# A hybrid decoder block on one core: halves of h stored side by side, and the first depth half of MLP units two to four in 512-column matmuls

## The chip, the core and the metric

The kernel runs on one core of a Trainium2 chip. The metric is the device time of one launch in microseconds; where a kernel was run several times, the median. A core has five engines that run side by side and meet through semaphores: TensorE (PE in the profile, with its weight loads shown apart as PEld), VectorE (DVE), ScalarE (ACT), GpSimd (POOL) and SyncE (SP, which here issues nearly all the loads). Each engine takes its instructions in the order in which they were written into its own list.

## The reference, cut to what matters

One decoder block in float32 on 256 positions and a width of 2048: an adaLN modulation computed from c, an S5 state-space branch beside block attention, a gated merge, and a squared-ReLU MLP of width 8192. The change lies in the MLP's first product; the layout of the first normed h changes too.

```python
mod = c_act @ w_ada[l] + b_ada[l]
sh1, sc1, g1, sh2, sc2, g2 = [m[:, None, :] for m in jnp.split(mod, N_MOD, axis=-1)]
...
h2 = rms_norm(x, norm_mlp_g[l]) * (1.0 + sc2) + sh2
x = x + g2 * (jnp.square(jax.nn.relu(h2 @ w_ff1[l])) @ w_ff2[l])
```

## The kernel before

Every float32 product is made from two rounded parts: a = a_hi + a_lo, and the product is taken as hi*hi + hi*lo + lo*hi. A weight tile of 128 x 1024 numbers (512 KB) is loaded by SP into one of seven buffers `wraw`. ACT casts it to `whi` (line 161) and DVE subtracts to get `wlo` (line 163); of each of these there are four buffers. `stream` does this ahead of the matmuls, under a raised priority. The activations h are held the same way, as a high half `ah` and a low half `al` of one buffer `a2` (tag A2), written by `make_h1` for the first sub-layer and by `make_h` for the MLP (in the trace: `ah` and `h2h`).

Two helpers multiply with a weight tile as the stationary operand, so that the result comes out transposed (hidden units on the partitions, 256 positions along the columns):

- `gemm_t` (lines 190 to 207) takes one depth tile of 128 rows and 1024 hidden units. Each block of 128 units gets three matmuls of 256 columns: whi with the high half of h, whi with the low half, wlo with the high half (lines 201, 202, 203). Two blocks share a bank of PSUM, four banks hold the result. One weight tile costs 24 matmuls.
- `gemm_d` (lines 209 to 231) takes two depth tiles and 512 hidden units. Each block gets one matmul of 512 columns, whi with both halves of h (line 219), and one of 256, wlo with the high half (line 223). A block has a bank to itself, with the products of the high half and of the low half in its two halves; they are added when the bank is emptied. One weight tile costs 8 + 8 matmuls. In a group's last weight tile the blocks are finished one after the other.

PSUM has eight banks: five (tag mm) for these results, three (tag ax) for small things. While the first depth half runs, a group of four takes four of the five; from the second depth half on, groups take turns between the two kinds.

The MLP has eight units of 1024 hidden units. For the first four (NP), the first part of the depth (kt 0 to 7; for the first unit kt 0 to 3) is computed early, in the loop `for g in range(NP)`, and its result is kept in SBUF in a tile `part`, because the rest of h is not yet there. The first unit runs on h before its scaling by 1/rms and is scaled by DVE afterwards (line 1470). In this loop the lane "ada" gives, per weight tile, RM = 0.85 further tiles of the modulation weights (`in_wat_dram`): SP loads them into the same seven buffers and DVE multiplies and sums each (line 314, called an adaLN sum here). They yield the scale and shift without which the second part of h cannot be made. Also in this loop lie four broadcasts (`ada_bcast`, line 400) and 16 transposes for that second part (`make_h`, line 759). Then `ff1` computes the rest of the depth with `gemm_d`, adds `part` (lines 1360 and 1361), applies the squared ReLU, and `ff2` multiplies with the second weight.

The order of the instructions on each engine is fixed when the program is built: a scheduler picks, by priorities and by its own estimate of when things are ready, so the lists differ from the order of the code. In particular it may let PE do several weight tiles on one bank before it goes on to the next bank, when it believes the next bank is still being emptied.

Of the kernel before, what the change touches and what calls it, by code (L numbers as in the profile page):

```python
# [13 lines left out]
F32R = mybir.dt.float32r  # L14
# [5 lines left out]
P = 128  # L20
S = 256
D = 2048
KT = D // P
# [54 lines left out]
class Kern:  # L78
# [130 lines left out]
    def gemm_d(self, src, kts, c0, x2):  # L209
        nc = self.nc  # L210
        banks = self.four("pd")
        pairs = self.pairs(list(kts))
        n = len(pairs)
        for i, (ks, hi, lo) in enumerate(self.stream(src, pairs, c0)):
            last = i == n - 1
            cut = lambda blk, k: slice(512 * k + blk * P, 512 * k + (blk + 1) * P)

            def high(blk, k):
                nc.tensor.matmul(banks[blk], hi[:, cut(blk, k)], x2[:, :, ks[k], :], start=i + k == 0, stop=False,  # L219
                                 skip_group_check=True)  # L220

            def low(blk, k):
                self.mm = nc.tensor.matmul(banks[blk][:, S:2 * S], lo[:, cut(blk, k)], x2[:, 0, ks[k], :], start=False,  # L223
                                           stop=last and k == 1, skip_group_check=True)

            for blks in [(b,) for b in range(4)] if last else [range(4)]:
                for f in (high, low):
                    for blk in blks:
                        for k in range(2):
                            f(blk, k)  # L230
        return banks
# [694 lines left out]
    def body(self):  # L926
        nc, a, v = self.nc, self.a, self.nc.vector
# [25 lines left out]
        A2, B2 = self.col("A2", KT), self.col("B2", KT)  # L953
# [36 lines left out]
        win = a["w_in"][0]  # L990
        with self.tc.high_priority(offset=OF1):
            self.norm1()
            a2 = self.slot("A2", [P, 2, KT, S], F32R, name="ah")
            self.ah, self.al = a2[:, 0], a2[:, 1]
            parts0 = modn(0)
            for units, fold, last in parts0:
                for ld, tot in units:
                    ld()
            totals(parts0)
            self.scale1(0, n=1)  # L1000
            self.make_h1(0, A1, B1, 1)
            self.gates = [(None, self.acopy)]
            for i in range(4):
                self.ada_bcast(rc[:, 4 * i:4 * i + 4], self.cb[:, i * 512:(i + 1) * 512], turn=False)
            self.ssm_params()
# [176 lines left out]
        for i in range(1, 4):  # L1182
# [3 lines left out]
            banks = self.gemm_n(win, range(KT), c0, self.ah, self.al, mid={8: to_ssm} if i == 1 else {})  # L1186
# [32 lines left out]
        banks = self.gemm_t(a["w_glu"][0], range(8), 0, yy[:, 0], yy[:, 1])  # L1219
# [24 lines left out]
        for cg in range(2):  # L1244
            banks = self.gemm_n(a["w_proj_ssm"][0], range(8), cg * 1024, gg[:, 0], gg[:, 1])
# [14 lines left out]
        for cg in range(2):  # L1260
# [6 lines left out]
            banks = self.gemm_n(a["w_out"][0], range(KT), cg * 1024, mh, ml, tail=TW if cg else 1)  # L1267
# [22 lines left out]
        with self.hot():  # L1290
            ss2 = self.col("ss2", 2)
            self.pin(v.reduce_sum(ss2, sq.rearrange("p (t c) -> p t c", t=2), axis=AX.X))
            rs2 = self.rstd(ss2, 2, "r2")
            a2 = self.slot("A2", [P, 2, KT, S], F32R, name="h2h")
            self.ah, self.al = a2[:, 0], a2[:, 1]
            s0 = scale2(0, 0, None)
            s1 = scale2(1, 0, s0)
        self.gates = [(None, None)] * 4 + [(s1, self.sq_last)] * 2
# [34 lines left out]
        w1, w2 = a["w_ff1"][0], a["w_ff2"][0]  # L1333
# [122 lines left out]
        self.lanes["ada"][1] = 0.0  # L1456
        for g in range(NP):
            part = self.slot(("S4", "T", "SV", "S5")[g], [P, 4, 512], name="part")
            if g:
                banks = self.gemm_t(w1, range(0, 8), g * 1024, self.ah, self.al)  # L1460
            else:
                wh, wl = [self.slot(n, [P, 4, 1024], F32R, name="wf") for n in ("VT", "QT")]
                banks = self.gemm_t(w1, range(0, 4), 0, hp[:, 0], hp[:, 1], mid={2: h_first, 3: h_second},
                                    homes=[(wh[:, k, :], wl[:, k, :]) for k in range(4)])
            for b in range(4):
                if g:
                    nc.scalar.copy(part[:, b, :], banks[b])
                else:
                    with self.after(hs["h0"]):
                        v.tensor_mul(part[:, b, :].rearrange("p (k s) -> p k s", s=S),  # L1470
                                     banks[b].rearrange("p (k s) -> p k s", s=S),
                                     self.R[:, None, :].to_broadcast([P, 2, S]))
            parts.append(part)
            if g == 0:
                self.lanes["ada"][1] = RM
                self.agate = None
            if g == 1:
                scale2(2, 0, self.done[-1][0])
                scale2(3, 0, self.done[-1][0])
                self.ada_bcast(B2[:, 0:4], b2r, self.mm)  # L1480
# [63 lines left out]
```

## Time and profile before

| what | value |
|---|---|
| time, median of 3 runs | 1387.89 us (1386.99 to 1388.09) |
| the profiled execution's own time | 1388.54 us |
| its span, first to last instruction | 1386.8 us |
| mean granted TensorE clock | 0.995 |
| matmuls in the trace | 8338 |
| the loop over the first depth half, units two to four | 676.3 to 748.8 us |

The profile's first part gives each engine's busy time, its share of the span and its instructions. A row of a timeline reads: start in us, duration in us, engine, line, operation, what is written and from what, shape, count, and in brackets how long the engine was idle before it and what ended that. Ends of matmuls are modelled, so that successive rows of PE overlap; the distance between starts is the pace. A row of a table by lines gives total busy time, mean ns of one, idle time before and what ended it. SPq is SP's queue, where the loads are issued.

### The profile page before, as it was taken

The page shows a single profiled execution, that of the slowest core. Times are in us where ns is not written, and L with a number is a line of the kernel's source. Part 1 is how long each engine was busy: PE and PEld are TensorE (multiplying, and loading weights), DVE is VectorE, ACT ScalarE, POOL GpSimd, SP SyncE. Part 2 cuts the span into 40 slices and gives each one's busy share as a digit, 9 for nine tenths or more (in the row PEclk, how much of TensorE's full clock was granted, in tenths as well). Part 3 has the DMA queues.
Part 4 walks back from the last instruction along what each step waited for, and adds up shares of the span by engine and source line. Part 5 has one row for each costly group of instructions (what it writes and reads, how often), then busy time and mean ns, then how long its engine had stood idle before and what let it go on. Part 6 is the DMA issues. An engine that isn't in the chain of part 4 may idle for free.

```text
span 1386.8 us, 21589 instructions
## 1 busy us (share of the span) xinstructions
PE 1354.2 (98%) x8338; PEld 1173.9 (85%) x8338; DVE 1061.6 (77%) x1481; ACT 709.7 (51%) x956; POOL 42.6 (3%) x96
## 2 busy tenths in 40 slices
PE   6999999999999999999999999999999999999997
PEld 5888898988788898788999888888888888888885
DVE  6699998788798898987886976777666555555677
ACT  4464356346646743446455655444453453634543
POOL 1000000400002100000000000000000000000000
PEclk9999999999999999999999999999999999999999
DMA  9999965888457889898597878797878656566561
GB/s 372 380 403 370 338 218 169 267 297 316 138 177 218 303 289 338 286 398 289 195 378 236 292 243 253 246 256 279 254 233 241 206 187 197 183 195 195 176 202 66
DMA packets 112422, 356.43 MB, mean 257 GB/s; under 512 B 12240, under 2 KB 12272, under 8 KB 111904
## 3 DMA queue, kind: packets, MB, share of 16 engines
q1 hardware_dynamic: 109280, 348.96, 74.5%
q0 software_dynamic: 2896, 5.83, 1.4%
q8 instruction: 65, 1.06, 0.3%
q10 hardware_dynamic: 144, 0.26, 0.1%
q14 instruction: 37, 0.30, 0.1%
HBM read 350.79 MB, written 2.51 MB: 255 GB/s over the span
## 4 chain that ended last, share of the span: by engine, by line
PE 84%; DVE 7%; DMA 4%; ACT 3%; issue 1%; SPq 0%; DVEq 0%; ACTq 0%
PE pn L253 15%; PE pn L254 14%; PE pn L255 14%; PE pd L219 13%; PE pd L223 7%; PE pt L202 5%; PE pt L201 5%; PE pt L203 5%; DVE wlo L163 2%; DVE wraw L314 1%; DMA wraw<-in_w_out_dram 1%; DMA wraw<-in_w_proj_ssm_dram 1%; ACT whi L161 1%; PE ys L908 1%; PE rk L723 1%
## 5 line engine op out<-in xcount | busy, mean ns | idle before, releaser
L161 ACT CAST whi<-wraw 128x1024 fp32r<-128x1024 f32 x448 | 468.1, 1051 | 547.2 <-PE pn L254 222.2
L163 DVE TENSOR_TENSOR wlo<-wraw,whi 128x1024 fp32r<-128x1024 f32 x448 | 545.7, 1224 | 238.4 <-ACT whi L161 231.5
L219 PE MATMUL pd<-h2h,whi 128*128 128x512 f32 x800 | 208.9, 393 | 0.0
L253 PE MATMUL pn<-whi,ff 128*128 128x512 f32 x496 | 193.0, 389 | 0.0
L254 PE MATMUL pn<-whi,ff 128*128 128x512 f32 x496 | 193.0, 389 | 0.0
L255 PE MATMUL pn<-wlo,ff 128*128 128x512 f32 x496 | 191.6, 389 | 0.0
L219 PEld LDWEIGHTS pd<-h2h,whi 128*128 128x128 f32 x800 | 140.5, 189 | 21.7
L314 DVE SCALAR_TENSOR_TENSOR wraw<-wraw,cb 128x1024 f32<-128x1024 f32 x128 | 156.2, 1221 | 0.0
L253 PE MATMUL pn<-whi,ah 128*128 128x512 f32 x320 | 126.4, 398 | 3.3 <-ACT ah L161 1.6
L223 PEld LDWEIGHTS pd<-h2h,wlo 128*128 128x128 f32 x800 | 116.1, 190 | 12.5
L254 PE MATMUL pn<-whi,ah 128*128 128x512 f32 x320 | 125.1, 391 | 0.0
L223 PE MATMUL pd<-h2h,wlo 128*128 128x256 f32 x800 | 119.3, 281 | 0.0
L255 PE MATMUL pn<-wlo,ah 128*128 128x512 f32 x320 | 114.6, 393 | 0.0
L201 PE MATMUL pt<-ah,whi 128*128 128x256 f32 x384 | 106.8, 287 | 6.3 <-ACT ah L161 4.5
L255 PEld LDWEIGHTS pn<-wlo,ff 128*128 128x128 f32 x496 | 93.1, 188 | 19.3
L253 PEld LDWEIGHTS pn<-whi,ff 128*128 128x128 f32 x496 | 93.1, 188 | 19.2
L254 PEld LDWEIGHTS pn<-whi,ff 128*128 128x128 f32 x496 | 93.1, 188 | 19.1
L202 PE MATMUL pt<-ah,whi 128*128 128x256 f32 x384 | 108.3, 287 | 0.0
L203 PE MATMUL pt<-ah,wlo 128*128 128x256 f32 x384 | 104.0, 286 | 1.5 <-DVE wlo L163 1.5
L201 PEld LDWEIGHTS pt<-ah,whi 128*128 128x128 f32 x384 | 73.5, 194 | 7.5 <-ACT ah L161 5.2
L202 PEld LDWEIGHTS pt<-ah,whi 128*128 128x128 f32 x384 | 74.3, 193 | 1.3 <-issue 0.8
L203 PEld LDWEIGHTS pt<-ah,wlo 128*128 128x128 f32 x384 | 71.9, 193 | 2.6 <-DVE wlo L163 2.3
(377 smaller groups left out, 1992.2 us busy)
## 6 DMA issues: line engine op xcount, KB each, us to landing
wraw<-in_w_ff_dram SPq DMA_DIRECT2D x256, 512.0 KB, 4.9
wraw<-in_w_in_dram SPq DMA_DIRECT2D x128, 512.0 KB, 6.2
wraw<-in_wat_dram SPq DMA_DIRECT2D x128, 512.0 KB, 5.5
ahm<-in_wat_dram SPq DMA_DIRECT2D x48, 512.0 KB, 7.3
wraw<-in_w_out_dram SPq DMA_DIRECT2D x32, 512.0 KB, 6.6
wraw<-in_w_proj_attn_dram SPq DMA_DIRECT2D x16, 512.0 KB, 5.9
wraw<-in_w_proj_ssm_dram SPq DMA_DIRECT2D x16, 512.0 KB, 6.5
ahm<-in_wan_dram SPq DMA_DIRECT2D x8, 512.0 KB, 11.0
```

The lines of the kernel that those rows point to most:

```text
L161: h = self.nc.scalar.copy(hi, src)
L163: s = self.nc.vector.tensor_sub(lo, src, hi.bitcast(F32))
L201: nc.tensor.matmul(o, hi[:, c], xh[:, kx, :], start=st, stop=False, skip_group_check=True)
L202: nc.tensor.matmul(o, hi[:, c], xl[:, kx, :], start=False, stop=False, skip_group_check=True)
L203: self.mm = nc.tensor.matmul(o, lo[:, c], xh[:, kx, :], start=False, stop=sp, skip_group_check=True)
L219: nc.tensor.matmul(banks[blk], hi[:, cut(blk, k)], x2[:, :, ks[k], :], start=i + k == 0, stop=False, skip_group_check=True)
L223: self.mm = nc.tensor.matmul(banks[blk][:, S:2 * S], lo[:, cut(blk, k)], x2[:, 0, ks[k], :], start=False, stop=last and k == 1, skip_group ...
L253: nc.tensor.matmul(o, xh[:, kx, tk], hi[:, c], start=q == 0, stop=False)
L254: nc.tensor.matmul(o, xl[:, kx, tk], hi[:, c], start=False, stop=False)
L255: self.mm = last = nc.tensor.matmul(o, xh[:, kx, tk], lo[:, c], start=False, stop=q == n - 1)
L314: v.scalar_tensor_tensor(w, w, 1.0, self.cb[:, (i % 2) * 1024:(i % 2 + 1) * 1024], op0=OP.mult, op1=OP.mult, accum_out=pc[:, i:i + 1])
L723: nc.tensor.matmul(p[q, k * 64:(k + 1) * 64], nr[q, i, k].rearrange("p s c -> p (s c)"), self.cc[q, i, 8 * b + k].rearrange("p s c -> p (s ...
```

## The change

`a2` is laid out as [partition, depth tile, half, position] instead of [partition, half, depth tile, position], in both places where it is made, so that the two halves of a depth tile lie side by side and the operand of line 219 is one run of 512 columns. The first depth half of MLP units two to four is computed by `gemm_d` in two groups of 512 hidden units each, instead of by one `gemm_t` of 1024. A group's four banks are emptied by an ACT copy of 256 columns and a DVE add of 256 columns each, where before ACT copied each bank whole. The first unit stays as it was.

```diff
--- before.py
+++ after.py
@@ -216,11 +216,11 @@
             cut = lambda blk, k: slice(512 * k + blk * P, 512 * k + (blk + 1) * P)
 
             def high(blk, k):
-                nc.tensor.matmul(banks[blk], hi[:, cut(blk, k)], x2[:, :, ks[k], :], start=i + k == 0, stop=False,
+                nc.tensor.matmul(banks[blk], hi[:, cut(blk, k)], x2[:, ks[k], :, :], start=i + k == 0, stop=False,
                                  skip_group_check=True)
 
             def low(blk, k):
-                self.mm = nc.tensor.matmul(banks[blk][:, S:2 * S], lo[:, cut(blk, k)], x2[:, 0, ks[k], :], start=False,
+                self.mm = nc.tensor.matmul(banks[blk][:, S:2 * S], lo[:, cut(blk, k)], x2[:, ks[k], 0, :], start=False,
                                            stop=last and k == 1, skip_group_check=True)
 
             for blks in [(b,) for b in range(4)] if last else [range(4)]:
@@ -990,8 +990,8 @@
         win = a["w_in"][0]
         with self.tc.high_priority(offset=OF1):
             self.norm1()
-            a2 = self.slot("A2", [P, 2, KT, S], F32R, name="ah")
-            self.ah, self.al = a2[:, 0], a2[:, 1]
+            a2 = self.slot("A2", [P, KT, 2, S], F32R, name="ah")
+            self.ah, self.al = a2[:, :, 0], a2[:, :, 1]
             parts0 = modn(0)
             for units, fold, last in parts0:
                 for ld, tot in units:
@@ -1291,8 +1291,8 @@
             ss2 = self.col("ss2", 2)
             self.pin(v.reduce_sum(ss2, sq.rearrange("p (t c) -> p t c", t=2), axis=AX.X))
             rs2 = self.rstd(ss2, 2, "r2")
-            a2 = self.slot("A2", [P, 2, KT, S], F32R, name="h2h")
-            self.ah, self.al = a2[:, 0], a2[:, 1]
+            a2 = self.slot("A2", [P, KT, 2, S], F32R, name="h2h")
+            self.ah, self.al = a2[:, :, 0], a2[:, :, 1]
             s0 = scale2(0, 0, None)
             s1 = scale2(1, 0, s0)
         self.gates = [(None, None)] * 4 + [(s1, self.sq_last)] * 2
@@ -1456,16 +1456,17 @@
         self.lanes["ada"][1] = 0.0
         for g in range(NP):
             part = self.slot(("S4", "T", "SV", "S5")[g], [P, 4, 512], name="part")
-            if g:
-                banks = self.gemm_t(w1, range(0, 8), g * 1024, self.ah, self.al)
-            else:
+            for h in range(2) if g else ():
+                banks = self.gemm_d(w1, range(0, 8), g * 1024 + 512 * h, a2)
+                for b in range(4):
+                    q = part[:, 2 * h + b // 2, (b % 2) * S:(b % 2 + 1) * S]
+                    nc.scalar.copy(q, banks[b][:, S:2 * S])
+                    v.tensor_add(q, q, banks[b][:, 0:S])
+            if g == 0:
                 wh, wl = [self.slot(n, [P, 4, 1024], F32R, name="wf") for n in ("VT", "QT")]
                 banks = self.gemm_t(w1, range(0, 4), 0, hp[:, 0], hp[:, 1], mid={2: h_first, 3: h_second},
                                     homes=[(wh[:, k, :], wl[:, k, :]) for k in range(4)])
-            for b in range(4):
-                if g:
-                    nc.scalar.copy(part[:, b, :], banks[b])
-                else:
+                for b in range(4):
                     with self.after(hs["h0"]):
                         v.tensor_mul(part[:, b, :].rearrange("p (k s) -> p k s", s=S),
                                      banks[b].rearrange("p (k s) -> p k s", s=S),
```

In the new program the copies are on line 1463 and the adds on line 1464; what was line 1470 is 1471.

PE's list in unit three before (pt0 to pt3 are the four banks, 7104 and 7137 the third and fourth weight tile of the unit):

```order
L201 MATMUL pt3_7031<-h2h_6563,whi_7104 128x256
L202 MATMUL pt3_7031<-h2h_6563,whi_7104 128x256
L203 MATMUL pt3_7031<-h2h_6563,wlo_7105 128x256
L201 MATMUL pt0_7028<-h2h_6563,whi_7137 128x256
L202 MATMUL pt0_7028<-h2h_6563,whi_7137 128x256
L203 MATMUL pt0_7028<-h2h_6563,wlo_7138 128x256
```

A weight tile is used on all four banks, and then comes the next one.

PE's list at the second group of unit three after the change (pd0_7093 and pd1_7094 are its first two banks, 7099, 7124, 7149 and 7174 its four weight tiles; the first row is the end of the group before):

```order
L223 MATMUL pd3_6983<-h2h_6563,wlo_7066 128x256 x2
L219 MATMUL pd0_7093<-h2h_6563,whi_7099 128x512 x2
L223 MATMUL pd0_7093<-h2h_6563,wlo_7100 128x256 x2
L219 MATMUL pd0_7093<-h2h_6563,whi_7124 128x512 x2
L223 MATMUL pd0_7093<-h2h_6563,wlo_7125 128x256 x2
L219 MATMUL pd0_7093<-h2h_6563,whi_7149 128x512 x2
L223 MATMUL pd0_7093<-h2h_6563,wlo_7150 128x256 x2
L219 MATMUL pd0_7093<-h2h_6563,whi_7174 128x512 x2
L219 MATMUL pd1_7094<-h2h_6563,whi_7099 128x512 x2
```

The first bank takes three weight tiles and the high part of the fourth before the second bank takes its first one. Banks three and four follow later, side by side. Of the six groups, the first takes its first two tiles bank by bank and the others tile by tile; the other five begin as shown. In the second and third group the last bank comes by itself at the end, with all its tiles; in the fourth to sixth it runs side by side with the third. The second depth half goes tile by tile again after its first group.

DVE's list in unit three before (wlo is a low part of a weight tile, wraw_...,pc an adaLN sum):

```order
L163 TENSOR_TENSOR wlo_7138<-wraw_7135,whi_7137 128x1024
L959 TENSOR_TENSOR A2_115<-pcs_7098,cols_90 128x4
L163 TENSOR_TENSOR wlo_7168<-wraw_7165,whi_7167 128x1024
L314 SCALAR_TENSOR_TENSOR wraw_7132,pc_328<-wraw_7132,cb_95 128x1024
L960 SCALAR_TENSOR_TENSOR A2_115<-A2_115,cols_90 128x4
L163 TENSOR_TENSOR wlo_7201<-wraw_7198,whi_7200 128x1024
L314 SCALAR_TENSOR_TENSOR wraw_7195,pc_328<-wraw_7195,cb_95 128x1024
L163 TENSOR_TENSOR wlo_7234<-wraw_7231,whi_7233 128x1024
```

And at the second group of unit three after the change:

```order
L163 TENSOR_TENSOR wlo_7100<-wraw_7097,whi_7099 128x1024
L314 SCALAR_TENSOR_TENSOR wraw_7060,pc_328<-wraw_7060,cb_95 128x1024
L163 TENSOR_TENSOR wlo_7125<-wraw_7122,whi_7124 128x1024
L314 SCALAR_TENSOR_TENSOR wraw_7119,pc_328<-wraw_7119,cb_95 128x1024
L163 TENSOR_TENSOR wlo_7150<-wraw_7147,whi_7149 128x1024
L314 SCALAR_TENSOR_TENSOR wraw_7144,pc_328<-wraw_7144,cb_95 128x1024
L1464 TENSOR_TENSOR part_6979<-part_6979,pd0_6980 128x256
L1464 TENSOR_TENSOR part_6979<-part_6979,pd1_6981 128x256
L1464 TENSOR_TENSOR part_6979<-part_6979,pd2_6982 128x256
L1464 TENSOR_TENSOR part_6979<-part_6979,pd3_6983 128x256
L163 TENSOR_TENSOR wlo_7175<-wraw_7172,whi_7174 128x1024
```

Between the low parts there are adaLN sums as before, and now the four adds of the group before stand ahead of the fourth low part. Each add waits for an ACT copy, and the matmuls that reuse its bank wait for the add.

## Prediction

> **What bounds the kernel now.** I read the page's first part, then a table of windows over the changed stage, then the timelines of PE, DVE and ACT in it. The first part:
>
> ```profile
> PE 1354.2 (98%) x8338; PEld 1173.9 (85%) x8338; DVE 1061.6 (77%) x1481; ACT 709.7 (51%) x956; POOL 42.6 (3%) x96
> ```
>
> TensorE (PE) is busy nearly all the time, so time is lost or won where PE gets more or less work, or has to wait. The changed stage (first depth half of MLP units two to four) runs from 676.3 to 748.8 us. Its windows (length; busy time of PE, PEld, DVE, ACT, POOL; granted clock; DMA share; GB/s):
>
> ```profile
> 676.30:700.40 24.10, 23.19 (x190) 22.58 (x189) 20.09 (x29) 11.27 (x15) 0.00 (x0) 1.00 0.69 249
> 700.40:724.50 24.10, 24.10 (x205) 24.10 (x203) 21.03 (x30) 13.99 (x19) 0.00 (x0) 1.00 0.99 374
> 724.50:748.80 24.30, 24.30 (x206) 24.30 (x205) 13.31 (x16) 13.44 (x18) 0.00 (x0) 1.00 0.79 267
> ```
>
> PE is idle for 0.9 us of 72.5. DVE is busy 41.1 of the first 48.2 us, so it is the next engine in line; in the last window it has room. The clock is full throughout.
>
> **The price of a matmul.** Busy time overlaps, so I take start to start. First three PE rows of the stage, then the weight loads of one of its three lines, then ACT's casts of the weights, which follow PE's pace there:
>
> ```profile
> 676.50 0.28 PE L202 MATMUL pt<-h2h,whi 128*128 128x256 f32 x1
> 676.62 0.28 PE L203 MATMUL pt<-h2h,wlo 128*128 128x256 f32 x1
> 676.73 0.28 PE L201 MATMUL pt<-h2h,whi 128*128 128x256 f32 x1
> ```
> ```profile
> L202 PEld LDWEIGHTS pt<-h2h,whi 128*128 128x128 f32 x192 | 36.8, 192 | 0.0
> ```
> ```profile
> 731.49 1.05 ACT L161 CAST whi<-wraw 128x1024 fp32r<-128x1024 f32 x1 [1.33 <-PE pt L202]
> 734.37 1.05 ACT L161 CAST whi<-wraw 128x1024 fp32r<-128x1024 f32 x1 [1.82 <-PE pt L202]
> 737.25 1.05 ACT L161 CAST whi<-wraw 128x1024 fp32r<-128x1024 f32 x1 [1.83 <-PE pt L202]
> ```
>
> A 256-column matmul takes 0.12 us, and a weight tile (24 of them) 2.88 us: the casts are that far apart. The new form already runs elsewhere in this kernel, in the second depth half. Its pace, first in a tile's ordinary order, then bank by bank:
>
> ```profile
> 1102.11 2.00 PE L219 MATMUL pd<-h2h,whi 128*128 128x512 f32 x8
> 1103.95 1.12 PE L223 MATMUL pd<-h2h,wlo 128*128 128x256 f32 x8
> 1104.90 2.00 PE L219 MATMUL pd<-h2h,whi 128*128 128x512 f32 x8
> ...
> 1110.48 0.63 PE L219 MATMUL pd<-h2h,whi 128*128 128x512 f32 x2
> 1110.95 0.39 PE L223 MATMUL pd<-h2h,wlo 128*128 128x256 f32 x2
> 1111.18 0.62 PE L219 MATMUL pd<-h2h,whi 128*128 128x512 f32 x2
> ```
>
> A tile takes 1104.90-1102.11 = 2.79 us, or 4 x 0.70 = 2.80 bank by bank; a pair of high matmuls 0.46, a pair of low ones 0.24. So 192 matmuls fewer are worth only 24 tiles x (2.88-2.80) = **1.9 us**: what goes is one weight load in three, and it was nearly hidden.
>
> A rule of the Trainium skill says otherwise: TensorE: Matmul & The Clock Gate, section "The mechanism", has weight loads overlap running matmuls only when the row groups differ; then each removed load would be saved whole. The trace disagrees: full 128-row matmuls start 120 ns apart though one load is shown as 192 ns long.
>
> **The halves side by side.** The high matmul now reads 512 columns in one run. With two runs, eight take 1103.95-1102.11 = 1.84 us, 0.230 each. Matmuls with an unbroken 512-column operand, with ten starts from the first to the last of these rows:
>
> ```profile
> 1150.02 0.39 PE L253 MATMUL pn<-whi,ff 128*128 128x512 f32 x1
> ...
> 1152.29 0.39 PE L254 MATMUL pn<-whi,ff 128*128 128x512 f32 x1
> ```
>
> That is 0.227. The most to gain is 0.003 x 800 high matmuls of the second depth half = 2.4 us. I take 0, since nothing shows that the two runs make the difference. The writers of h now store 2x256 pieces; a DVE add with a permuted destination costs what one without costs:
>
> ```profile
> L1051 DVE TENSOR_TENSOR uT<-uT,pt 128x512 f32<-128x512 f32 x8 | 5.0, 684 | 0.0
> L1042 DVE TENSOR_TENSOR v<-v,pn 128x512 f32<-128x512 f32 x8 | 5.0, 681 | 0.0
> ```
>
> I take 0 for that as well, and for the readers of ah, whose operands keep their widths.
>
> **What is added.** Twelve ACT copies of 512 become 24 of 256, and DVE gets 24 adds. Rows of DVE (start, us) and of ACT:
>
> ```profile
> 683.39 1.23 DVE L163 TENSOR_TENSOR wlo<-wraw,whi 128x1024 fp32r<-128x1024 f32 x1 [0.26 <-ACT whi L161]
> 684.53 1.22 DVE L314 SCALAR_TENSOR_TENSOR wraw<-wraw,cb 128x1024 f32<-128x1024 f32 x1
> 685.67 1.22 DVE L163 TENSOR_TENSOR wlo<-wraw,whi 128x1024 fp32r<-128x1024 f32 x1
> ...
> 772.66 1.42 DVE L1360 TENSOR_TENSOR part<-part,pd 128x256 f32<-128x256 f32 x4
> ```
> ```profile
> 682.31 2.94 ACT L161 CAST whi<-wraw 128x1024 fp32r<-128x1024 f32 x3
> 689.80 2.16 ACT L161 CAST whi<-wraw 128x1024 fp32r<-128x1024 f32 x2 [4.54 <-PE pt L203]
> 694.04 1.05 ACT L161 CAST whi<-wraw 128x1024 fp32r<-128x1024 f32 x1 [2.08 <-DMA wraw<-in_w_ff_dram]
> ```
>
> A low part (call it a sub) and an adaLN sum each take DVE 1.14 us, an add about 0.33, a cast 0.95 (1.05 until it can be used). The adds are 24 x 0.33 = 8 us, on top of 54.4 busy in some 70: as a total they fit. ACT is busy 11 to 14 us of 24, so its twelve more copies cost 0. SP issues the same loads in the same order; weights now come as two rows of 512 columns, as in the second depth half, where PE keeps its 2.79: 0. Weight tiles and 0.85 adaLN tiles of 0.524 MB per 2.80 us ask for 346 GB/s, under the 374 above. So neither DVE nor DMA becomes the bound as a total; the order does the harm.
>
> **Where PE will wait.** Before, PE finished a tile on all banks before the next, so the four buffers of whi and wlo came free one by one and ACT and DVE ran tiles ahead. In the new order (section on the change) five of the six halves go bank by bank: the first bank asks for three or four tiles within 2 us, and all four stay held until the last bank has used them. Also, with five banks for groups of four, the second bank of a half waits for DVE's add of the half before. Behind each sub on DVE the next adaLN sum is queued. Call the halves A to F, E the end of the half before, tiles 1 to 4.
>
> Half D, for which the order is shown. In half C the last bank takes tiles 1, 2, 3 whole, then the low passes of tile 4 on three banks (0.71), then its own tile 4: tile 1 comes free at E-2.8, its whi at E-3.05. Cast until E-2.0, sub until E-0.85, sum until E+0.3, sub 2 until E+1.45, sum until E+2.6, sub 3 until about E+3.8, sum until E+4.9, first add E+5.25. PE: tile 1 until E+0.7, high of tile 2 until 1.16, wait for sub 2 (0.3), then to 2.2 with the high of tile 3, wait for sub 3 (1.6), low and high until 4.5, wait for the add that frees bank two (0.75). **2.7 us.**
>
> Half E: half D frees its tile 1 earlier, at E-4.2 (whi E-4.45), because its banks three and four run side by side. All above shifts by 1.4, and no sum stands between sub 3 and the adds: one wait of about **0.6**. Half F: no sums are left between the subs: 0. Half C: 16 transposes and four broadcasts run inside it, and four transposes take 0.35:
>
> ```profile
> 674.91 0.60 PE L759 MATMUL trh<-ident,xs 128*128 128x128 f32 x4
> 675.26 0.36 PE L202 MATMUL pt<-hp,wf 128*128 128x256 f32 x1
> ```
>
> They push PE's need for sub 2 from 1.16 to 2.6 us after E, and sub 2 is there at 1.45: 0. Half B: PE takes up tile 3 of half A at 683.4 (the cast of 682.31), two tiles bring it to 689.0, B1 on one bank to 689.7. Tile B2 is the one cast at 689.80 in the old run; its load could only be issued when DVE's sub of 683.39 had freed a buffer:
>
> ```profile
> 684.64 1.47 SPq L156 DMA_DIRECT2D wraw<-in_w_ff_dram  x2
> ```
>
> DVE is as late then after the change, since its order is the same up to that sub. Cast until 690.85, sub until 692.0; PE wants it at 690.15: **1.9 us**. B4, landed by 694.04, is in time. Half A: as before PE waits for the first unit's evacuation and for the cast at 682.31:
>
> ```profile
> L201 PE MATMUL pt<-h2h,whi 128*128 128x256 f32 x192 | 54.3, 286 | 0.9 <-ACT whi L161 0.5 <-DVE part L1470 0.3
> ```
>
> Its tiles are now used up a little sooner: 0.3 more. **Sum:** 0.3+1.9+2.7+0.6 = 5.5 of waits, less 1.9 of matmul time, **+3.6 us**. Nothing later takes it back, as PE is the bound to the end. Bounds of the waits: 0, if lookahead covers all, and 2.7 at each of the five changes of half plus 0.3, 13.8, as the worst one; I am nearer to the walk than to either.
>
> The profiled execution took 1388.54 us (span 1386.8); with +3.6 it would be 1392.1. The median before is 1387.89, 0.65 lower, so I forecast **1391.5**.
>
> **Rivals.** *PE stays fed.* DVE idles some 18 of 72 us in this stage, and before it hid as many subs without a wait. For it: the adds fit. Against it: the buffers' late release. Then the time is 1387.89-1.9 = 1386.0, and with the full 2.4 of the unbroken reads 1383.6. It wins if the third sub of a half is done within 1.9 us of the half before, that is with no sum between two subs. 0.27. *The waits spread.* A late sub delays the freeing of load buffers (seven), the loads then come late as at 694.04, and each change of half costs what the worst costs: 13.8-1.9 = +11.9, 1399.8. Against it: the last third of the stage has DVE idle 11 of 24 us. 0.08. *Loads not hidden.* If every removed weight load (192 x 192 ns) stood on the path, -36.9, 1351.0; against it stand the 120 ns. 0.03. (This is what the Trainium skill's rule above, in TensorE: Matmul & The Clock Gate, section "The mechanism", would give.)
>
> **How the numbers follow.** My forecast has 0.62, with its own range of about +1 to +8 (waits of 3 to 10). What a measurement here can tell from no change is 0.2%, 2.8 us. Slower by more: 0.49 of my case and the 0.08, 0.57. Same: 0.13 of my case and 0.20 of the fed one, 0.33. Faster: 0.07 of the fed one with part of the read gain, and 0.03: 0.10. The range for 8 in 10 runs from the fed case without read gain, 1386.0, to +8, 1395.9.
>
> **What would show it.** The first matmul of the second depth half stands here:
>
> ```profile
> 749.26 0.70 PE L219 MATMUL pd<-h2h,whi 128*128 128x512 f32 x2
> ```
>
> Right: it starts about 3.6 us later; PE's idle time in the stage grows from 0.9 to about 6 us, ended by DVE's wlo and by the part adds, most of it at the start of half D; ACT's casts come in bursts of three, ended by PE. Wrong: PE idles under 2 us in the stage (then it is fed), or waits mostly for DMA (then the waits spread), or high matmuls below 0.227 us.

## The result, and the profile after

| | before | after |
|---|---|---|
| time, median of 5 runs beside each other | 1387.89 us (1386.99 to 1389.10) | 1395.41 us (1392.53 to 1396.75) |
| profiled execution, and its span | 1388.54, 1386.8 us | 1395.19, 1393.3 us |
| PE busy, matmuls in the trace | 1354.2 us, 8338 | 1354.5 us, 8146 |

The ratio is 1.0054, with a 95% interval of 1.0043 to 1.0065: slower by 6.0 to 9.0 us. A second set of runs, on another chip (below, the change again), gave 1.0029 (1.0017 to 1.0041), 2.4 to 5.7 us. The forecast was +3.6, with a range up to +8.

The windows over the changed stage, after (columns as before):

```profile
676.30:700.40 24.10, 20.88 (x117) 17.54 (x116) 20.36 (x36) 12.02 (x19) 0.00 (x0) 1.00 0.69 237
700.40:724.50 24.10, 21.13 (x125) 17.46 (x124) 19.51 (x34) 13.83 (x23) 0.00 (x0) 1.00 0.86 291
724.50:748.80 24.30, 23.63 (x137) 20.41 (x136) 19.35 (x30) 13.04 (x22) 0.00 (x0) 1.00 0.88 311
```

PE is idle for 72.5-65.64 = 6.9 us where it was idle for 0.9. DVE is busy 39.9 of the first 48.2 us, no more than before. In the last 24.3 us, where it had room, it is busy 19.35 in place of 13.31. So no engine is full; there are waits. Here are all the starts of PE in the stage ahead of which it was idle for over 0.1 us:

```profile
679.53 0.73 PE L219 MATMUL pd<-h2h,whi 128*128 128x512 f32 x2 [1.31 <-DVE h2h L163]
685.23 2.12 PE L219 MATMUL pd<-h2h,whi 128*128 128x512 f32 x8 [0.56 <-ACT whi L161]
693.33 0.51 PE L223 MATMUL pd<-h2h,wlo 128*128 128x256 f32 x2 [1.08 <-DVE wlo L163]
696.91 1.66 PE L219 MATMUL pd<-h2h,whi 128*128 128x512 f32 x6 [0.28 <-ACT whi L161]
707.26 0.66 PE L759 MATMUL trh<-ident,xs 128*128 128x128 f32 x4 [0.59 <-ACT b2r L403]
720.00 0.50 PE L223 MATMUL pd<-h2h,wlo 128*128 128x256 f32 x2 [0.48 <-DVE wlo L163]
722.28 0.50 PE L223 MATMUL pd<-h2h,wlo 128*128 128x256 f32 x2 [1.31 <-DVE wlo L163]
723.85 0.70 PE L219 MATMUL pd<-h2h,whi 128*128 128x512 f32 x2 [0.60 <-DVE part L1464]
735.23 0.50 PE L223 MATMUL pd<-h2h,wlo 128*128 128x256 f32 x2 [0.67 <-DVE wlo L163]
```

The first two lie in half A, then two in B, one in C, three in D, one in E, none in F. Half D went step by step as the walk in the prediction had it: a wait for sub 2, one for sub 3, one for the add that frees bank two. ACT's casts and DVE's list there, after:

```profile
715.35 2.95 ACT L161 CAST whi<-wraw 128x1024 fp32r<-128x1024 f32 x3 [1.26 <-PE pd L219]
```
```profile
716.44 1.23 DVE L163 TENSOR_TENSOR wlo<-wraw,whi 128x1024 fp32r<-128x1024 f32 x1 [1.62 <-ACT whi L161]
717.58 1.22 DVE L314 SCALAR_TENSOR_TENSOR wraw<-wraw,cb 128x1024 f32<-128x1024 f32 x1
...
718.73 1.22 DVE L163 TENSOR_TENSOR wlo<-wraw,whi 128x1024 fp32r<-128x1024 f32 x1
719.87 1.22 DVE L314 SCALAR_TENSOR_TENSOR wraw<-wraw,cb 128x1024 f32<-128x1024 f32 x1
...
721.01 1.22 DVE L163 TENSOR_TENSOR wlo<-wraw,whi 128x1024 fp32r<-128x1024 f32 x1
722.15 1.22 DVE L314 SCALAR_TENSOR_TENSOR wraw<-wraw,cb 128x1024 f32<-128x1024 f32 x1
...
723.29 1.40 DVE L1464 TENSOR_TENSOR part<-part,pd 128x256 f32<-128x256 f32 x4
```

Three casts in one burst, released by PE alone, then a sub, a sum, a sub, a sum, a sub, a sum, and only then the adds. Each of PE's three waits in D ends with one of these rows. No wait of PE in the stage is ended by a load directly; behind two of them stands a cast that had itself waited for its load (tiles two and four of half B).

**The stage alone.** The profiled executions also differ ahead of the stage, where the program is the same. To take that out I use one window for each kernel, from just behind the start of one and the same cast, the first of the first unit's weights (653.93 before, 655.76 after), to 3.3 us ahead of one and the same cast of the second depth half (813.33 before, 819.79 after). Its length less that of before is what the stage cost. Before, then after:

```profile
654.00:810.00 156.00, 155.09 (x1092) 145.25 (x1092) 126.61 (x195) 90.88 (x128) 0.00 (x0) 1.00 0.79 275
```
```profile
655.83:816.47 160.64, 153.78 (x897) 133.58 (x896) 133.75 (x219) 90.81 (x140) 0.00 (x0) 1.00 0.77 267
```

So the stage cost 160.64-156.00 = 4.6 us; the casts were the other 1.8 of the span's 6.5 late when the window opened. PE itself was less late there. Its first row of the first unit's product, before and then after, is 0.99 us later, not 1.83:

```profile
657.91 0.28 PE L201 MATMUL pt<-hp,wf 128*128 128x256 f32 x1
```
```profile
658.90 0.28 PE L201 MATMUL pt<-hp,wf 128*128 128x256 f32 x1
```

The difference of 0.84 us comes back inside the stage, as part of PE's first wait (see half A below).

### The profile page after: what moved, and what is told of

The parts are those of the page before. It is cut to its first block, busy times and chain, and to the rows that moved or that the text cites. A ratio compares the mean times of both kernels' runs of the same rounds, so it can differ in the third digit from the quotient of the medians.

```text
span 1393.3 us, 21249 instructions
## 1 busy us (share of the span) xinstructions
PE 1354.5 (97%) x8146; PEld 1164.3 (84%) x8146; DVE 1068.2 (77%) x1505; ACT 709.7 (51%) x968; POOL 42.7 (3%) x96
## 4 chain that ended last, share of the span: by engine, by line
PE 83%; DVE 9%; DMA 3%; ACT 3%; issue 2%; DVEq 0%; SPq 0%; ACTq 0%
PE pn L253 15%; PE pn L254 15%; PE pn L255 15%; PE pd L219 15%; PE pd L223 8%; PE pt L202 4%; PE pt L201 4%; PE pt L203 4%; DVE wlo L163 3%; DVE wraw L314 2%; DMA wraw<-in_w_out_dram 1%; ACT whi L161 1%; DMA wraw<-in_w_ff_dram 1%; PE ys L908 1%; PE rk L723 1%
## 5 line engine op out<-in xcount | busy, mean ns | idle before, releaser
L219 PE MATMUL pd<-h2h,whi 128*128 128x512 f32 x992 | 266.3, 394 | 2.7 <-DVE h2h L163 1.3
L219 PEld LDWEIGHTS pd<-h2h,whi 128*128 128x128 f32 x992 | 171.3, 189 | 27.2 <-DVE h2h L163 1.5
L223 PEld LDWEIGHTS pd<-h2h,wlo 128*128 128x128 f32 x992 | 148.6, 190 | 23.7 <-DVE wlo L163 5.3
L223 PE MATMUL pd<-h2h,wlo 128*128 128x256 f32 x992 | 154.4, 282 | 3.5 <-DVE wlo L163 3.5
```

The costliest lines, as they stand in the source:

```text
L219: nc.tensor.matmul(banks[blk], hi[:, cut(blk, k)], x2[:, ks[k], :, :], start=i + k == 0, stop=False, skip_group_check=True)
```

## The experiments

Theory: PE's new order, bank by bank, holds all four buffers and banks, so that subs and adds come late on DVE. Rivals: the layout; the 8 us of adds on DVE by themselves; the transfers. The stage's cost is always the length of the window just described, less 156.0.

### The layout alone

The kernel before, with `a2 = self.slot("A2", [P, KT, 2, S], ...)` and the operands that go with it, and `gemm_t` for units two to four.

> The kernel before with one part of the change: h's halves side by side per depth tile ([P, KT, 2, S]), while units two to four keep the three 256-column matmuls per block. Theory (the cost comes from the new order of matmuls in the stage, which holds the cast buffers): no more than 0.1% from before, and the first matmul of the stage within 0.5 us of 676.3. Rival (the layout costs or shifts something, as the changed kernel's 1.0 us later start of the stage could mean): about +1 us, with the stage again starting near 677.3. If unbroken operands were read faster, about -2 us, with eight high matmuls of the second depth half in 1.82 us in place of 1.84.

Measured: ratio 0.9999 (0.9987 to 1.0011). The window of the stage:

```profile
652.40:808.40 156.00, 155.16 (x1093) 145.31 (x1092) 126.79 (x195) 91.09 (x128) 0.00 (x0) 1.00 0.79 275
```

The stage costs 0.0. The weight casts stand 1.60 us ahead of those of before when the window opens, and still 1.60 at 1303 us, so 800 high matmuls with an unbroken operand gained nothing. The first matmul of the stage stands at 674.76, not within 0.5 us of 676.3 as expected; but this offset comes from ahead of the stage, and it went the other way than the rival had it. The layout is out as a cause.

### The matmuls alone

The changed kernel with the old layout, `x2[:, :, ks[k], :]` as the operand.

> The changed kernel with the old layout [P, 2, KT, S]: the 512-column matmuls of units two to four read two runs of 256. Its engines' order is the changed kernel's. Theory (order and buffers): +5.5 to +7.5 us over before, the same waits in the stage. Rival (the layout is part of the loss): +4 to +5. If the unbroken read is worth something, it is slower than the changed kernel by up to 3 us.

Measured: 1.0039 (1.0025 to 1.0053), +5.4 us.

```profile
654.06:814.60 160.54, 155.68 (x900) 135.11 (x899) 133.79 (x219) 90.85 (x140) 0.00 (x0) 0.99 0.78 266
```

The stage costs 4.5, and the waits are among those of the changed kernel: 0.67 and 0.56 in A, 1.08 in B, 0.48 and 1.31 in D, 0.66 in E, 4.8 us. The loss belongs to the matmuls' part of the change. The ratio lies between what the theory (from +5.5) and the rival (up to +5) gave, and does not tell them apart; the layout-alone run does. (The clock of 0.99 is a dip behind the waits of D, worth 1.7 us; without it the stage would have cost 2.8. The wait of 0.60 us for an add, just behind, is not there in this run. On dips see the last section.)

### Tile by tile

```diff
-    def gemm_d(self, src, kts, c0, x2):
+    def gemm_d(self, src, kts, c0, x2, keep=lambda i: i):
...
+                keep(self.mm)
...
-                banks = self.gemm_d(w1, range(0, 8), g * 1024 + 512 * h, a2)
+                banks = self.gemm_d(w1, range(0, 8), g * 1024 + 512 * h, a2, keep=self.pin)
```

`self.pin` holds an instruction to the order of the code (the high matmuls are kept too).

> The changed kernel with the matmuls of units two to four kept in the order in which the loop writes them: each weight tile on all four banks before the next, the last tile bank by bank. Theory (bank by bank order holds all four buffers and calls for four tiles within 2 us): PE's idle time in the stage falls from about 6.5 to 1 to 2 us, among it the wait for h's second piece, and the time is -1.5 to +1 us against before. Rival (DVE's load, the adds, sets the pace): PE waits as much, only spread over more tiles, +4 to +7. Rival (transfers): PE waits for loads, +4 or more.

Measured: 1.0024 (1.0014 to 1.0033), +3.3 us; the stage costs 159.76-156.00 = 3.8. The theory was right that the waits for subs go, and wrong in the total, 4.6 us of waits where it had 1 to 2. PE's waits in the stage are these three and no others:

```profile
677.64 1.93 PE L219 MATMUL pd<-h2h,whi 128*128 128x512 f32 x6 [1.07 <-DVE part L1472]
691.18 1.19 PE L219 MATMUL pd<-h2h,whi 128*128 128x512 f32 x4 [1.79 <-DVE part L1465]
694.13 0.80 PE L219 MATMUL pd<-h2h,whi 128*128 128x512 f32 x2 [1.76 <-DVE part L1465]
```

Every wait for a sub is gone, those of D and E with them, while the adds and sums on DVE stay: without the bank-by-bank order there are no such waits. In their place PE waits for banks at the start of half B, where a tile wants all four at once and only one is spare. DVE's list there:

```profile
689.58 1.22 DVE L163 TENSOR_TENSOR wlo<-wraw,whi 128x1024 fp32r<-128x1024 f32 x1
690.72 0.74 DVE L1465 TENSOR_TENSOR part<-part,pd 128x256 f32<-128x256 f32 x2
691.38 1.21 DVE L163 TENSOR_TENSOR wlo<-wraw,whi 128x1024 fp32r<-128x1024 f32 x1
692.51 1.22 DVE L315 SCALAR_TENSOR_TENSOR wraw<-wraw,cb 128x1024 f32<-128x1024 f32 x1
...
693.66 0.74 DVE L1465 TENSOR_TENSOR part<-part,pd 128x256 f32<-128x256 f32 x2
```

Half A's four adds, 0.33 us each, stand in two pairs behind a sub and a sum each. The bank is released not by the 0.33 us but by the queue ahead of it. Of the stage's 3.8 us, 1.7 are a dip of the clock behind these waits (0.83 from 692 to 696 us, 0.74 from 696 to 700: 0.43 x 4).

### Without the adds

```diff
                     nc.scalar.copy(q, banks[b][:, S:2 * S])
-                    v.tensor_add(q, q, banks[b][:, 0:S])
```

> The changed kernel without the 24 adds on DVE: it leaves out the product with the high half of h in the first depth half of units two to four (only the other part of each bank is copied out). Theory (order and buffers): the waits for late low parts stay, those for a bank's release go; 1 to 3 us faster than the changed kernel, +4 to +6 against before. Rival (the 8 us of adds on DVE are the loss): no slower than before, -2 to +1.

Measured: 0.9991 (0.9981 to 1.0001), -1.2 us; the stage costs 154.31-156.00 = -1.7. This is what the rival said. But, as PE's rows show (eight high matmuls in a run), with banks released by ACT the scheduler also writes PE's list nearly tile by tile, so the run takes away two things at once: DVE's 8 us and DVE's say over the banks. The next two tell these apart. It also shows the matmuls' price: with 0.9 us of waits left, as many as before, -1.7 is close to the -1.9 worked out for 192 matmuls fewer.

### Banks emptied by ACT, adds from SBUF

```diff
+            if g == 1:
+                scr = self.slot("VT", [P, 2, 4, 512], name="scr")
...
-                    nc.scalar.copy(q, banks[b][:, S:2 * S])
-                    v.tensor_add(q, q, banks[b][:, 0:S])
+                    nc.scalar.copy(scr[:, h, b, :], banks[b])
+                    v.tensor_add(q, scr[:, h, b, 0:S], scr[:, h, b, S:2 * S])
```

> The changed kernel with a different evacuation: ACT copies each whole bank (512 columns) into a free piece of SBUF, and DVE adds the two halves there, so that a bank comes free without DVE. The order on PE is then the scheduler's for that, nearly tile by tile after the first half. Theory (order, then bank release by DVE): idle time of PE in the stage 1 to 2.5 us, all of it in half A and at the start of B; through the stage -1 to +0.5 us, the time -2 to +1 against before. Rival (8 us of adds on DVE make the subs late, wherever they read): PE waits for wlo as in the changed kernel, +4 to +6.

Measured: 0.9990 (0.9981 to 0.9998), -1.4 us; the stage costs 154.83-156.00 = -1.2. DVE does the same 24 adds, and the waits for subs are gone:

```profile
674.79 0.73 PE L219 MATMUL pd<-h2h,whi 128*128 128x512 f32 x2 [0.71 <-DVE h2h L163]
680.50 2.11 PE L219 MATMUL pd<-h2h,whi 128*128 128x512 f32 x8 [0.57 <-ACT whi L161]
689.49 0.73 PE L219 MATMUL pd<-h2h,whi 128*128 128x512 f32 x2 [0.81 <-ACT scr L1465]
```

The mean add takes 419 ns here and 412 in the changed kernel. So DVE's load is not the cause. What this run changes is who releases the banks, and with it the order.

### Both: tile by tile, and banks emptied by ACT

> Matmuls kept tile by tile, and the banks evacuated by ACT alone as in the run with ACT copies. Theory: the two waits of 1.8 us for the part adds in the pinned run go, what stays is 1 us for unit one's evacuation in half A; through the stage -1.9+1 = about -1, the time -2 to +0.5 against before. Rival (DVE's load): +3 or more, PE waiting for wlo.

Measured: 0.9997 (0.9988 to 1.0006); the stage costs 155.35-156.00 = -0.7. Of the pinned run's waits the one for unit one's evacuation is left, and one for ACT's copy stands in the place of the two of 1.8 us:

```profile
677.86 1.93 PE L219 MATMUL pd<-h2h,whi 128*128 128x512 f32 x6 [1.22 <-DVE part L1474]
691.47 0.73 PE L219 MATMUL pd<-h2h,whi 128*128 128x512 f32 x2 [0.70 <-ACT scr L1466]
```

This is as the theory said, but for the 0.7. The order is the same in both runs, so here the release alone is changed: 3.55 us of waits for it against 0.70.

### Four more buffers

```diff
+                if h:
+                    wh, wl = [self.slot(n, [P, 4, 1024], F32R, name="wf") for n in ("VT", "QT")]
+                    homes = [(wh[:, k, :], wl[:, k, :]) for k in range(4)]
```

> The changed kernel with four more buffers for whi and wlo in halves B, D and F (in SBUF that is free in this stage); evacuation with the adds as in the change. Theory (held buffers make the subs late): the waits for wlo at the start of D and E (2.5 us) go, those for a bank's release stay: +2 to +4 against before. Rival (buffers do not matter, DVE's load does): the waits for wlo stay, +5 to +7.

Measured: 1.0063 (1.0050 to 1.0076), +8.7 us; the stage costs 163.80-156.00 = 7.8. A miss in size. The waits for subs at D and E did go, as the theory said; but with the new buffers the scheduler now writes half B's first two tiles ahead of half A's last two, in ACT's list and in PE's:

```profile
687.76 1.12 PE L219 MATMUL pd<-h2h,wf 128*128 128x512 f32 x2 [3.65 <-ACT wf L161]
697.61 0.50 PE L223 MATMUL pd<-h2h,wf 128*128 128x256 f32 x2 [0.29 <-DVE wf L163]
700.67 0.73 PE L219 MATMUL pd<-h2h,wf 128*128 128x512 f32 x2 [2.56 <-DVE part L1468]
```

```profile
686.67 1.04 ACT L161 CAST wf<-wraw 128x1024 fp32r<-128x1024 f32 x1 [0.82 <-DMA wraw<-in_w_ff_dram]
...
688.14 1.99 ACT L161 CAST whi<-wraw 128x1024 fp32r<-128x1024 f32 x2
```

PE stands 3.65 us before a tile of B whose load lands late, with A's two tiles cast behind it, and then 2.56 us for an add; the clock dips behind both. More buffers did not help by themselves.

### The change again

> The changed kernel once more, beside the three others. Through the stage +4.5 us, as in its first profile (6.47 at the end less 1.83 at the first weight casts of the stage), whatever the offset at the stage's start: that offset went from -1.6 to +1.8 in runs whose code ahead of the stage is equal, so it should come out different here. Rival (the new layout shifts the stage's start by +1 to +2): that offset is +1 to +2 again. The time +4.5 to +7.5 against before.

Measured: 1.0029 (1.0017 to 1.0041), +4.0 us, median 1391.99 of 11 runs.

```profile
651.16:810.99 159.83, 154.64 (x901) 134.38 (x900) 133.79 (x219) 90.76 (x140) 0.00 (x0) 1.00 0.78 267
```

The time is below the +4.5 to +7.5 expected. The stage costs 3.8 in place of 4.5, and it was entered 2.8 us earlier than before, not later: the layout does not shift it. B, D and E have the waits of the first profile within 0.1 us; A's wait for h is 0.31 instead of 1.31, and C has none.

### Half B on other banks

```diff
+                self.turn = True if (g, h) == (1, 1) else None
                 banks = self.gemm_d(w1, range(0, 8), g * 1024 + 512 * h, a2)
+                self.turn = None
```

This is on top of the run with banks emptied by ACT.

> The run with ACT copies of whole banks, and half B on the four banks that are not half A's (three of them from the pool of transposes), so that no half B matmul waits for half A's evacuation. Theory: the 0.8 us wait for ACT's copy at the start of half B goes, waits left are 0.3 to 0.7 for h's second piece and 0.57 for the cast of 682; through the stage -1.5 to -2.0 us, the time -3 to 0 against before. Rival (the wait only moves, to the low part of half B's second tile): through the stage -1.2, as without it.

Measured: 0.9986 (0.9976 to 0.9996), -1.9 us; the stage costs 153.73-156.00 = -2.3. One wait is left in the whole stage, and it was there before the change:

```profile
682.39 2.11 PE L219 MATMUL pd<-h2h,whi 128*128 128x512 f32 x8 [0.56 <-ACT whi L161]
```

This version is a little faster than the kernel before, by 0.14% with an interval just clear of 1: the 1.9 us of matmul time, and 0.3 of the 0.9 us of old waits. The wait for h, which was expected to stay, is not there; that it is missing is chance, as half A below shows.

### Unit two in the old form

`for h in range(2) if g > 1 else ():`, and for `g == 1` the lines before the change.

> The changed kernel with unit two in the old form (24 matmuls of 256 columns per tile, copies without adds), units three and four as in the change. Theory (each half's waits add up on their own): the waits of halves A and B go back to 0.9 us in all, those of D (2.4) and E (0.7) stay; through the stage 16 tiles x -0.08 + 3.1 = +1.8 us, the time +1 to +3. Rival (a lateness handed on from half to half): without A and B's waits those of D shrink as well, through the stage -1 to 0.

Measured: 0.9998 (0.9987 to 1.0008); the stage costs 154.64-156.00 = -1.4. Here the theory was wrong and the rival's mechanism right, with a stage still a little faster than its range: with A and B in the old form the waits of D and E are gone too, and what is left is before's 0.33 and 0.53 us in unit two. PE goes nearly tile by tile in halves C to F of this kernel (at 720.16 us, say, eight high matmuls in one run, and then eight low ones), although DVE's adds still release their banks. So the order of a half is not a property of the half, nor of the release alone; it changes with the halves ahead of it. Whether the old order with these later halves would have waited could not be separated from that.

### Fewer adaLN sums

`self.lanes["ada"][1] = 0.4` in place of RM in the stage.

> The changed kernel with adaLN sums at 0.4 per tile in place of 0.85 in this stage; those left run when the stage is over. The scheduler's order of the matmuls shifts a little with it. Theory (a sum queued on DVE between two subs makes the second and third sub late): PE's waits for wlo at the start of halves B to E fall from 3.5 to under 1.5 us in all, and those for a bank's release to under 0.5; +1 to +3 through the stage, unless the sums moved behind it cost there. Rival (the adds alone, or the order alone): the waits for wlo stay at 3 or more.

Measured: 1.0014 (1.0004 to 1.0025), +1.9 us; the stage costs 157.43-156.00 = 1.4. In the six halves PE waits once, for a sub, at the start of B, and never for a bank (the first row). The second depth half begins at 747.58 us, after a wait of 0.37 for a cast, and the next two rows already lie in it:

```profile
690.78 0.50 PE L223 MATMUL pd<-h2h,wlo 128*128 128x256 f32 x2 [0.38 <-DVE wlo L163]
```
```profile
748.99 0.50 PE L223 MATMUL pd<-h2h,wlo 128*128 128x256 f32 x2 [0.69 <-DVE wlo L163]
756.18 1.66 PE L219 MATMUL pd<-h2h,whi 128*128 128x512 f32 x6 [1.66 <-ACT whi L161]
```

So at 747.58 the run is 1.7 us ahead of before (749.26), and loses more than that behind the stage, where the sums that are left meet subs and casts. The waits came out as the theory said. But the order changed more than expected: in half C PE goes tile by tile (eight high matmuls in one run at 701.40 us, then eight low ones), as in the run with unit two in the old form. Sums and order went together, so this run does not show what the sums cost by themselves. That they stand between the subs is read from DVE's rows of half D above.

## Why the prediction was right, and where it was off

The sign was right, and so was the mechanism: subs and adds late at the changes of half, worst in D. The sum over the stage was nearly right. The median of the first set, +7.5, lies just inside the range and is twice the forecast; the second set, +4.0, is close to it. Waits of PE by half, in us (A's predicted value is the 0.9 of before and the 0.3 added to it):

| half | predicted | after | the change again |
|---|---|---|---|
| A | 1.2 | 1.87 | 0.88 |
| B | 1.9 | 1.36 | 1.26 |
| C | 0 | 0.59 | 0 |
| D | 2.7 | 2.39 | 2.38 |
| E | 0.6 | 0.67 | 0.67 |
| F | 0 | 0 | 0 |
| sum, less the 0.9 of before | 5.5 | 6.0 | 4.3 |
| the stage's cost, window to window | 3.6 | 4.6 | 3.8 |

That the sums come so close is in part luck: B and D came out smaller than predicted, and each wait cost PE about 0.16 us more than its bracket says, which the prediction did not count. From start to start, less the pace, the eight waits of the repeat cost 6.5 us in place of 5.2, and the two of before 1.2 in place of 0.9. Less the 1.9 of matmul time this gives 3.4 of the 3.8. The largest share of the waits is at D, as forecast, but with 2.4 of 6.9 us it is not most of them.

- *The price of a matmul, -1.9.* Right: the stage costs -1.7 without the adds and -2.3 with all new waits gone. Had the removed loads stood on the path, it would have been -36.9. The Trainium skill (TensorE: Matmul & The Clock Gate, section "The mechanism") allows a second case that the prediction left out: a load into the background weight buffer also runs ahead of matmuls in flight. The small gain here, 1.7 to 2.3 us for 192 loads, agrees with that case, and not with the one by row groups alone.
- *The unbroken reads, 0.* Right: 0.0 over the layout-alone run.
- *The adds fit as a total.* Right, and by the run with adds from SBUF shown, not only argued: DVE's work is the same there, and the loss is gone.
- *Half D, 2.7.* Right in each step: 0.48, 1.31 and 0.60 us against 0.3, 1.6 and 0.75. Half E too, 0.67 against 0.6.
- *Half B, 1.9.* Mis-sized: 1.08 for the second tile's sub and 0.28 for the fourth's cast, which the prediction had in time. The sub ended 1.2 us later than in the walk (693.2 for 692.0), behind an adaLN sum; but PE, held in A, came 1.9 us later (692.1 for 690.15).
- *Half A, "used up a little sooner: 0.3 more".* This step was wrong in the first profile. Its new wait is for h itself: a tile of `gemm_d` holds two depth tiles, and PE's list goes to the second weight tile, so to depth tiles two and three, 0.7 us after the first one, where it had 5.8 us (two tiles of 2.88) before. The prediction didn't ask when the moving operand is ready. The wait took 1.31 us there and 0.31 in the repeat, and this difference is not the change's. The casts, and the pieces of h with them, entered the stage 1.83 us later than before in the one and 2.84 sooner in the other; PE 0.99 later and 2.68 sooner. So h was 0.84 us late against PE in the one, and 0.16 early in the other. In all six runs in which PE waits for h here, the wait is 0.47 us plus this lateness, to 0.01 us. Without it half A would have about 1.0 us of waits, near the 1.2.
- *Half C, 0.* 0.59 us in one profile, for ACT's copy of the broadcasts ahead of the transposes (`b2r`); none in the repeat.
- *"It starts about 3.6 us later."* The second depth half's first matmul moved from 749.26 to 755.81, by 6.55 us: 4.6 from the stage, and 1.8 brought in from ahead of it, 0.99 by PE itself and 0.84 by h. That part is not the stage's.

```profile
755.81 0.63 PE L219 MATMUL pd<-h2h,whi 128*128 128x512 f32 x2
```

What the prediction did not see is that the waits hang together. It took the order on PE as given, and it saw two costs of it: held buffers and late adds. Put tile by tile (the pinned run), the waits for subs go, and the DVE release costs PE 3.6 us of waits at the start of half B; with ACT's release in that same order it costs 0.7. Where ACT releases the banks, the scheduler leaves the bank-by-bank order by itself; but it does so, too, with DVE's release, when unit two is in the old form or the sums are fewer. So the release is one reason for the order, and not the only one. Not run was the changed kernel's order with ACT's release, nor the adds put ahead of the subs in DVE's list.

Its rival "PE stays fed" came true once ACT copied 512 columns in place of 256 and half B had banks of its own (-1.9 us by the ratio, against the -1.9 given for it): the condition it named, no sum between subs, was not the only way there.

Open is the distance between the two sets of runs, 1.0054 and 1.0029 with intervals that do not meet: the stage explains 3.8 to 4.6 us in either profile. The dip of the clock in the first (last section) does not explain the rest: it cost 1.7 us, but near the program's start the clock is at half for 6.83 us in before and for only 3.41 in after, as in the repeat. Why all five runs of the first set lie high was not settled.

## What to carry to other kernels

Price a bank's release by the whole queue of the engine that empties it, not by the length of the instruction: a 0.33 us add behind a sub and a sum held PE for 1.8 us, twice. Let an engine with room copy the bank out whole, and do arithmetic from SBUF; and when a loop takes two depth tiles at once, ask when its moving operand is ready, too. A list that a scheduler writes depends on such releases and on what runs ahead of them, so an order read off for one version is no constant of the code: unit two's old form changed the order of halves C to F.

## What the runs showed of the hardware

A wait of PE can cost nearly twice its length. At 225 us, long before the changed stage, PE waits 1.74 to 1.75 us in before, after and the repeat alike. Here is the start that ends it, with the windows behind it; first after:

```profile
227.09 0.39 PE L201 MATMUL pt<-ah,whi 128*128 128x256 f32 x1 [1.74 <-DVE ga L1065]
```
```profile
228.00:232.00 4.00, 4.00 (x23) 4.00 (x22) 3.10 (x4) 0.00 (x0) 0.00 (x0) 0.57 0.23 45
```

And before:

```profile
227.81 0.39 PE L201 MATMUL pt<-ah,whi 128*128 128x256 f32 x1 [1.75 <-DVE ga L1065]
```
```profile
228.00:232.00 4.00, 4.00 (x35) 4.00 (x35) 3.82 (x5) 0.00 (x0) 0.00 (x0) 1.00 0.10 22
```

After, the granted clock is 0.57 over four microseconds, 0.50 from 228.22 to 231.63, and 23 matmuls run where 35 did: (1-0.57) x 4 = 1.7 us lost. The row that ends the wait stood 0.72 us sooner in after than in before, and the profile of after brought 1.8 us into the stage; the dip is 1.7 of these 2.55 us, and the rest was not traced. With this wait the clock stays at 1.00 in before and in the repeat; over all, it drops there in six of the thirteen profiles of this study, with and without the change.

It is not blind chance which six. In each profile, all the half-clocked stretches begin at whole multiples of 3.413 us from the first one (I call these times marks); in after they begin at 23.42 and at 228.22, 60 multiples apart. The wait of after, 225.35 to 227.09, lies whole between two marks, 224.81 and 228.22. In the repeat, whose first stretch begins at 23.68, a mark at 225.07 cuts the wait of 224.53 to 226.28 in two. In six of the thirteen profiles the wait is cut by a mark, and the clock drops in none of them. In seven it lies between two marks, and the clock drops in six; in the seventh (four more buffers) the wait begins on a mark within 0.02 us. The rule is not complete, for in the pinned run one wait of 1.79 us between two marks (687.80 and 691.22) passed without a drop, and the next, of 1.76, was followed by one. The first stretch begins between 21.46 and 25.72 us in these profiles, so where a wait will fall is still luck.

The stage's own waits can be hit as well: in the matmuls-alone run, behind the waits of 0.48 and 1.31 us in half D, the clock is

```profile
720.00:724.00 4.00, 3.91 (x14) 2.79 (x14) 4.00 (x8) 0.00 (x0) 0.00 (x0) 0.61 0.97 336
```

and in the changed kernel, behind the same waits, 1.00. There a mark at 719.74 cuts the first of them; in the matmuls-alone run both lie between 716.28 and 719.69. This puts a wait's expected price above its length, and widens the spread of the runs.

The Trainium skill (TensorE: Matmul & The Clock Gate, section "What's actually happening") has a free-running window of about 3.4 us, and half clock after an idle one. The dips agree with it in depth (0.50), in length (3.41 us) and in the marks 3.41 us apart, whatever the kernel does. They disagree with it in that no such window was idle as a whole, and with the section "HAM oscillation — how this bites in real kernels", by which idle gaps matter above about 3.4 us: here one gap of 1.74 us was followed by the half clock, and so was one of 0.48 with one of 1.31 close behind it.
